# One core's decoder layer: negated rstd kept in the rstd's tile, first weights loaded ahead of x and the norm's scale, nine matmuls on zeros

## The chip, the cores and the metric

One core of a Trainium2 chip runs the whole layer. The metric is the time of one execution on the device in microseconds, of the slowest core, which here is the only one. Several executions are timed; one more is profiled, and all rows come from that one.

## The reference, cut to what matters

All tensors are float32; x is 512 x 2048.

```python
h = rms_norm(x, norm_gain)
q, k, v, g_attn, c_b, c_c, c_h, g_conv = split(h @ w_in)         # 2048 -> 6656
q, k = partial_rope(rms_norm(q, ...)), partial_rope(rms_norm(k, ...))
y_attn = sliding_window_attention(q, k, v, sinks) * silu(g_attn)  # 16 heads of 64, window 128
y_conv = c_b * short_conv(c_c * c_h, conv_w) * silu(g_conv)
x = x + concat(y_attn, y_conv) @ w_out                            # 2048 -> 2048
gate = sigmoid(rms_norm(x, ple_gate_norm_gain) @ w_ple_gate + b)  # 2048 -> 2048
x = x + gate * rms_norm(p @ w_ple_proj, ple_norm_gain)
```

## The kernel before

**Precision.** Every float32 operand is split into a high part, rounded to the matmul's own format, and the rest, the low part (`wh` and `wl` of weights, `hsh` and `hsl` of the normed x, `form` for both). One product is three matmuls: high by high, low by high, high by low.

**Stages.** The head (lines 262 to 283) loads x in 16 tiles of 128 x 512 and the weights of k and v in 16 pieces of 256 KB, scales each x tile by the norm's gain (`norm_g`, the norm's scale) and splits it, and gathers k and v in four banks of PSUM (L274: wh stationary, hsh or hsl moving). The rstd itself is only applied to the products. Then `gemm_tile` (L155 to L157) makes 24 tiles of the input projection, with weights from `wsp` stationary and hs from `hsp` moving; attention (L448, L449, transposes L481, values L495 and L496) and the embedding's projection (`e_block`, L555) run in between. From about 386 us on, seven groups of block products (L845, a scheme with seven products for a 2 x 2 block) make the rest of the input projection (groups 0 to 2), the output projection (3, 4) and the gate (5, 6). There `form`, 128 x 128 pieces of the activations, is stationary and `wh` or `wl`, 128 x 512, is moving. A step is one of the forms 1 to 7 for one of four chunks of the rows, 12 matmuls. In groups 0 to 2 the forms are pieces of hs: forms 1, 2, 4 and 7 lie in `hsp`, forms 5, 6 and 3 in `fx`, but forms 6 and 3 of chunk 3 lie in `rowp` (`h_slot("rows" if j > 5 else "fx")`, L1282).

**Order.** TensorE's instructions stand in the order of the code throughout. ScalarE's and VectorE's do so in the first six rounds of the head and again in the block products; between, a scheduler sets them. SyncE and GpSimd issue the loads and stores, each in one queue. In a round of the head ScalarE makes `hsh` (L133), casts `wh` (L117) and squares x; VectorE makes `hsl` (L134) and `wl` (L118). `fetch` (L97 to L107) issues the loads of x and weights.

**Memory.** A pool is a stretch of every partition; its place follows from the sizes of the pools ahead of it. `const`, `small`, `hsp`, `wsp`, `wraw` and what replaces them (`fx`, `tab`, `ap`, `cw`) are stacked from the left; `rowp`, `big`, and the block products' `spl`, `wx`, `wy`, `ws`, `io_p`, `quad` from the right end. `r_neg` (L301) is a tile of 32 floats in `const` of which four are used: the rstd of x times -1/8, which `x_squared` writes and GpSimd reads for the scale of q.

**Start.** TensorE begins with ten products of a tile of zeros by itself (L187, L188); each stands as two records in the trace.

Of the kernel before, what the change touches and what calls it, by code (L numbers as in the profile page):

```python
# [9 lines left out]
F32 = mybir.dt.float32  # L10
F32R = mybir.dt.float32r
AF = mybir.ActivationFunctionType
ALU = mybir.AluOpType

P = 128
# [3 lines left out]
NB = T // P  # L19
HD = 64  # L20
# [10 lines left out]
def f32(ap):  # L31
    return ap.bitcast(F32)
# [3 lines left out]
def hymba_layer(ctx: ExitStack, tc: tile.TileContext, io):  # L36
# [14 lines left out]
    nc = tc.nc  # L51
# [3 lines left out]
    const = ctx.enter_context(tc.tile_pool(name="const", bufs=1))  # L55
# [15 lines left out]
    def cload(name, shape):  # L71
        t = const.tile(shape, F32, name=name)
        nc.gpsimd.dma_start(t, io[name])
        return t
# [6 lines left out]
    jobs = [io["w_kv"][i] for i in range(8)]  # L81
# [5 lines left out]
    raws, splits = {}, {}  # L87
    RAW_AHEAD, SPLIT_AHEAD = 2, 3

    xt = []  # L90

    def load_x():
        xt.append(big.tile([P, T], F32, tag="big", name="x"))
        nc.sync.dma_start(xt[-1], io["x"][len(xt) - 1])

    def fetch(s):

        for j in range(min(s // 2 + RAW_AHEAD + 1, len(jobs))):
            if j not in raws:
                raws[j] = wraw.tile([P, 8, P], F32, name="raw")  # L100
                if j < 8:
                    for c in (slice(0, 4), slice(4, 8)):
                        load_x()
                        nc.sync.dma_start(raws[j][:, c], jobs[j][:, c])
                else:
                    nc.sync.dma_start(raws[j], jobs[j])

# [16 lines left out]
    def split_tile(src, scale=None, name="s", pool=None):  # L124

        pool, tag = (big, "big") if pool is None else (pool, "h")
        h = pool.tile([P, T], F32R, tag=tag, name=name + "h")
        l = pool.tile([P, T], F32R, tag=tag, name=name + "l")
        if scale is None:
            nc.scalar.copy(h, src)  # L130
            nc.vector.tensor_tensor(l, src, f32(h), op=ALU.subtract)
        else:
            nc.scalar.activation(h, src, AF.Copy, scale=scale)  # L133
            nc.vector.scalar_tensor_tensor(l, src, scale, f32(h), op0=ALU.mult, op1=ALU.subtract)  # L134
        return h, l
# [5 lines left out]
    def at(when, fn):  # L141
        later.append((when, len(later), fn))
# [41 lines left out]
    nc.vector.memset(zeros, 0.0)  # L184
    nc.scalar.activation(half_neg[:, 31:], zeros[:, :1], AF.Copy, bias=-0.5)
    warm_ps = ps_o.tile([P, P], F32, name="pso")
    for _ in range(10):  # L187
        nc.tensor.matmul(warm_ps, zeros, zeros, start=True, stop=True)  # L188

    ind = const.tile([P, 2 * P], F32R, name="ind")  # L190
    for c in range(2):
        nc.vector.tensor_copy(ind[:, c * P : (c + 1) * P], zeros)
    norm_g = const.tile([P, KT], F32, name="norm_gain")
    nc.sync.dma_start(norm_g, io["norm_gain"])
    ident = cload("ident", [P, P])
    gate_g = cload("ple_gate_norm_gain", [P, KT])
    qg, kg = cload("q_norm_gain", [P, 2]), cload("k_norm_gain", [P, 2])
# [4 lines left out]
    def half_sums(pm, hl, t, first, last):  # L202

        w = ind[:, P - 2 * t : 2 * P - 2 * t]
        nc.tensor.matmul(pm, w, hl[0], start=first, stop=False)
        nc.tensor.matmul(pm, w, hl[1], start=False, stop=last)

    def take_rows(pm, rows):
        sb = big.tile([rows, T], F32, tag="big", name="rowsum")
        nc.scalar.copy(sb, pm[:rows])  # L210
        return sb

    def to_tokens(sb):

        rows = sb.shape[0]
        pt = ps_m.tile([P, T], F32, name="psm")
        out = pt[:, : NB * rows].rearrange("p (b r) -> p b r", r=rows)
        for b in range(NB):
            nc.tensor.transpose(out[:, b, :], sb[:, b * P : (b + 1) * P], ident[:rows, :rows])
        return out  # L220

    def rstd(ms, n, out):

        nc.vector.tensor_scalar(ms, ms, 1.0 / n, EPS, op0=ALU.mult, op1=ALU.add)
        width = int(np.prod(ms.shape[1:]))
        e = half_neg[:, :width]
        if len(ms.shape) == 3:
            e = e.rearrange("p (a b) -> p a b", a=ms.shape[1])
        nc.gpsimd.tensor_tensor(out, ms, e, op=ALU.pow)

    tok = {}

    def token_rstd(name, sq, out, when):


        def sums():
            pm = ps_o.tile([P, T], F32, name="pso")
            half_sums(pm, hl, 0, True, True)
            tok["s"] = take_rows(pm, 2)

        def turn():
            ms = small.tile([P, NB], F32, name="ms")
            nc.vector.tensor_reduce(ms, to_tokens(tok["s"]), axis=mybir.AxisListType.X, op=ALU.add)
            r = tok[name] = const.tile([P, NB], F32, name="r_" + name)
            rstd(ms, D, r)
            tok["rb"] = big.tile([P, NB, P], F32, tag="big", name="rb")
            nc.vector.tensor_copy(tok["rb"], r.unsqueeze(2).broadcast_to([P, NB, P]))

        def rows():
            pb = ps_m.tile([P, T], F32, name="psm")  # L250
            for b in range(NB):
                nc.tensor.transpose(pb[:, b * P : (b + 1) * P], tok["rb"][:, b, :], ident)
            nc.scalar.copy(out, pb)

        hl = split_tile(sq)
        for stage, t in zip((sums, turn, rows), when):
            at(t, stage)
# [32 lines left out]

    def x_squared():
        nc.vector.tensor_tensor(rx2_tok, tok["x"], tok["x"], op=ALU.mult)
        nc.vector.tensor_scalar(r_neg, tok["x"], -(HD**-0.5), None, op0=ALU.mult)
        nc.vector.tensor_tensor(rx2, rx, rx, op=ALU.mult)

    c0 = clock[0]
    token_rstd("x", acc, rx, (c0 + 3, c0 + 5, c0 + 8))
    at(c0 + 9, x_squared)

    attn_dram = [dram.tile([2 * P, T], F32, name=f"a{j}") for j in range(NKV)]  # L300
    r_neg = const.tile([P, 32], F32, name="r_neg")[:, :NB]  # L301
    conv_dram, mix_dram = ([dram.tile([P, T], F32, name=f"{n}{i}") for i in range(8)] for n in ("c", "m"))

    with ExitStack() as att:
# [16 lines left out]
        def squares(ps):  # L321
            sq = big.tile([P, T], F32, tag="big", name="sqh")
            nc.scalar.activation(sq, ps, AF.Square)
            return sq

        def head_scale(rows, out, r, engine):

            shape = [P, NB, rows.shape[0]]
            ms = small.tile(shape, F32, name="msh")
            nc.vector.tensor_tensor(  # L330
                ms, to_tokens(rows), rx2_tok.unsqueeze(2).broadcast_to(shape), op=ALU.mult
            )
            rstd(ms, HD, ms)
            return lambda: engine.tensor_tensor(out, ms, r.unsqueeze(2).broadcast_to(shape), op=ALU.mult)

        def rotate(ps, g):
            t1 = big.tile([P, T], F32, tag="big", name="rot")
            sh = cw.tile([P, T], F32, tag="cw", name="shf", bufs=4)
            nc.vector.stream_shuffle(sh, ps, shuf)
            nc.vector.scalar_tensor_tensor(t1, ps, g[:, 0:1], cos, op0=ALU.mult, op1=ALU.mult)  # L340
            nc.vector.scalar_tensor_tensor(sh, sh, g[:, 1:2], sin, op0=ALU.mult, op1=ALU.mult)
            nc.vector.tensor_tensor(t1, t1, sh, op=ALU.add)
            return t1
# [68 lines left out]
        def q_tile(t):  # L412
            ps = product()
            sq = split_tile(squares(ps))

            def sum_q():
                if t % 4 == 0:
                    tok["q"] = ps_o.tile([P, T], F32, name="pso")
                half_sums(tok["q"], sq, t % 4, t % 4 == 0, t % 4 == 3)
                if t % 4 == 3:  # L420
                    tok["q"] = take_rows(tok["q"], 8)

            def scale_q():
                sl = nscale[:, :, 2 * t - 6 : 2 * t + 2]
                head_scale(tok["q"], sl, r_neg, nc.gpsimd)()

            at(clock[0] + 6, sum_q)
            if t % 4 == 3:
                at(clock[0] + (9 if t == 3 else 17), scale_q)
            qr = rotate(ps, qg)  # L430
            for hf in range(2):
                own, oth = slice(hf * HD, hf * HD + HD), slice((1 - hf) * HD, (1 - hf) * HD + HD)
                st = big.tile([P, T], F32R, tag="big", name="qst")
                nc.scalar.copy(st[own], qr[own])
                nc.vector.tensor_tensor(st[oth], qr[own], f32(st[own]), op=ALU.subtract)
                qst[2 * t + hf] = st
# [74 lines left out]
        def product():  # L511

            i = tile_at[0]
            tile_at[0] += 1
            ps = gemm_tile(hs, mid=(lambda: e_block(E_AT.index(i))) if i in E_AT else None)
            for fn in busy.pop(i, ()):
                fn()
            return ps
# [860 lines left out]
```

## Time and profile before

| what | value |
|---|---|
| median of 3 runs | 953.41 us (952.49 to 954.28) |
| the profiled execution, its own time | 952.76 us |
| its span, first to last instruction | 951.0 us |
| granted TensorE clock, mean | 0.999 |
| TensorE, matmuls | 943.8 us busy, 4294 records |
| VectorE | 711.2 us busy |
| ScalarE | 524.8 us busy |
| GpSimd | 151.2 us busy |
| memory read and written | 197 GB/s over the span |

A record of a matmul lasts from its start to its modelled end and overlaps the next one's, so the pace of a stream is read from the distance of starts: in the chain in order of time, each piece with its count runs to the start of the next.

### The profile page before, as it was taken

Reading aid. Unit: us, or ns where it says so; the run is one execution under the profiler, and the core shown is the slowest. Engines: PE = TensorE matmul, PEld = TensorE weight load, DVE = VectorE, ACT = ScalarE, POOL = GpSimd, SP = SyncE. Lnnn points to the kernel's source line nnn. Section 1 sums busy time; section 2 is a strip of 40 time slices with the busy share of each in tenths; the row PEclk is TensorE's granted clock in tenths of the full one; section 3 lists DMA queues with packets and bytes.
Section 4 is the critical chain, followed back from the end, with each engine's and each line's share of the span. In section 5 each row is a group of like instructions: output and inputs, shape, how many; then the busy total and the mean of one; then the engine's idle time right before and its main releaser. Section 6 shows DMA issues by size and latency. Waiting matters only on the chain.

```text
span 951.0 us, 12360 instructions
## 1 busy us (share of the span) xinstructions
PE 943.8 (99%) x4294; PEld 775.1 (82%) x4294; DVE 711.2 (75%) x1104; ACT 524.8 (55%) x891; POOL 151.2 (16%) x200
## 2 busy tenths in 40 slices
PE   9999999999999999999999999999999999999997
PEld 7888888888888888888888888888888888888886
DVE  6778867975766676667667768988858686997678
ACT  7546555665656665345344446555657566664453
POOL 2002142051212221000100110011020112002101
PEclk9999999999999999999999999999999999999999
DMA  9434455564555657765824887787996895579956
GB/s 318 143 103 155 144 192 199 175 187 101 150 160 147 195 154 257 267 222 195 225 74 159 277 203 223 239 236 177 272 313 171 224 294 129 133 234 303 223 136 210
DMA packets 68078, 188.22 MB, mean 198 GB/s; under 512 B 8144, under 2 KB 14592, under 8 KB 68016
## 3 DMA queue, kind: packets, MB, share of 16 engines
q1 hardware_dynamic: 46336, 128.48, 39.6%
q0 software_dynamic: 21680, 58.96, 27.1%
q8 instruction: 33, 0.54, 0.2%
q14 instruction: 29, 0.24, 0.1%
HBM read 158.05 MB, written 29.36 MB: 197 GB/s over the span
## 4 chain that ended last, share of the span: by engine, by line
PE 98%; DVE 0%; DMA 0%; ACT 0%; SPq 0%; issue 0%
PE psp L845 53%; PE psg L155 9%; PE psg L157 9%; PE psg L156 9%; PE pst L845 4%; PE pss L274 2%; PE pst L274 2%; PE pst L911 1%; PE pst L481 1%; PE pst L555 1%; PE pss L555 1%; PE pss L449 1%; PE pss L448 1%; PE pso L496 1%; PE pso L495 1%; DMA raw<-in_w_kv 0%
## 5 line engine op out<-in xcount | busy, mean ns | idle before, releaser
L845 PE MATMUL psp<-wh,form 128*128 128x512 f32 x1056 | 331.6, 395 | 0.0
L845 PEld LDWEIGHTS psp<-wh,form 128*128 128x128 f32 x1056 | 197.9, 188 | 45.4
L845 PE MATMUL psp<-wl,form 128*128 128x512 f32 x528 | 208.4, 395 | 0.0
L155 PE MATMUL psg<-hsh,wh 128*128 128x512 f32 x384 | 152.0, 396 | 0.0
L157 PE MATMUL psg<-hsh,wl 128*128 128x512 f32 x384 | 149.9, 390 | 0.0
L156 PE MATMUL psg<-hsl,wh 128*128 128x512 f32 x384 | 149.8, 390 | 0.0
L812 DVE TENSOR_TENSOR wl<-wy,wh 128x1024 fp32r<-128x1024 f32 x84 | 102.5, 1222 | 52.3 <-ACT wh L811 52.3
L811 ACT CAST wh<-wy 128x1024 fp32r<-128x1024 f32 x84 | 88.0, 1048 | 85.1 <-PE psp L845 62.9
L118 DVE TENSOR_TENSOR wl<-raw,wh 128x512 fp32r<-128x512 f32 x120 | 82.2, 687 | 49.5 <-ACT wh L117 31.1
L845 PEld LDWEIGHTS psp<-wl,form 128*128 128x128 f32 x528 | 99.4, 188 | 23.2
L117 ACT CAST wh<-raw 128x512 fp32r<-128x512 f32 x120 | 73.6, 617 | 68.6 <-PE psg L156 51.6
L812 DVE TENSOR_TENSOR wl<-wx,wh 128x1024 fp32r<-128x1024 f32 x56 | 68.4, 1223 | 35.9 <-ACT wh L811 35.8
L811 ACT CAST wh<-ws 128x1024 fp32r<-128x1024 f32 x56 | 58.8, 1051 | 62.9 <-PE psp L845 38.2
L811 ACT CAST wh<-wx 128x1024 fp32r<-128x1024 f32 x56 | 58.6, 1049 | 61.5 <-PE psp L845 52.7
L812 DVE TENSOR_TENSOR wl<-ws,wh 128x1024 fp32r<-128x1024 f32 x56 | 68.5, 1223 | 25.3 <-ACT wh L811 25.1
L157 PEld LDWEIGHTS psg<-hsh,wl 128*128 128x128 f32 x384 | 72.1, 188 | 15.4
L155 PEld LDWEIGHTS psg<-hsh,wh 128*128 128x128 f32 x384 | 72.2, 188 | 14.1
L156 PEld LDWEIGHTS psg<-hsl,wh 128*128 128x128 f32 x384 | 72.2, 188 | 13.9
L845 PE MATMUL psp<-wh,hsh 128*128 128x512 f32 x192 | 76.1, 396 | 0.0
L845 PE MATMUL psp<-wh,hsl 128*128 128x512 f32 x192 | 75.8, 395 | 0.0
L845 PE MATMUL psp<-wl,hsh 128*128 128x512 f32 x192 | 75.7, 394 | 0.0
L797 DVE TENSOR_TENSOR wy<-wy,ws 128x1024 f32<-128x1024 f32 x56 | 68.2, 1217 | 0.4 <-DMA ws<-in_w_ple_gate 0.4
(223 smaller groups left out, 1353.3 us busy)
## 6 DMA issues: line engine op xcount, KB each, us to landing
raw<-in_w_in SPq DMA_DIRECT2D x48, 512.0 KB, 3.5
ws<-in_w_mid SPq DMA_DIRECT2D x24, 512.0 KB, 4.0
h<-hf POOLq DMA_DIRECT2D x32, 256.0 KB, 4.4
wx<-in_w_mid SPq DMA_DIRECT2D x16, 512.0 KB, 4.2
wx<-in_w_out SPq DMA_DIRECT2D x16, 512.0 KB, 5.3
ws<-in_w_out SPq DMA_DIRECT2D x16, 512.0 KB, 5.4
ws<-in_w_ple_gate SPq DMA_DIRECT2D x16, 512.0 KB, 5.3
wy<-in_w_mid SPq DMA_DIRECT2D x12, 512.0 KB, 6.8
```

Source lines behind the costliest of these rows:

```text
L117: nc.scalar.copy(wh, raw)
L118: nc.vector.tensor_tensor(wl, raw, f32(wh), op=ALU.subtract)
L155: nc.tensor.matmul(ps, wh, ah, start=first, stop=False)
L156: nc.tensor.matmul(ps, wh, al, start=False, stop=False)
L157: nc.tensor.matmul(ps, wl, ah, start=False, stop=last)
L274: nc.tensor.matmul(kv_ps[t], w[:, t, :], a, start=k == 0 and i == 0, stop=k == KT - 1 and i == 2)
L448: nc.tensor.matmul(sc[:, r, lo:], q, khh[j][:, ks], start=True, stop=False)
L555: nc.tensor.matmul(banks[t], a, w, start=k == 0 and i == 0, stop=k == 1 and i == 2)
L797: tt(y, y, got[g, "s1" if f == 6 else "s0", c], op=ALU.add)
L811: nc.scalar.copy(wh, src)
L812: tt(wl, src, f32(wh), op=ALU.subtract)
L845: nc.tensor.matmul(ps[t], a, w[:, i], start=start and first and i == 0 and n == 0, stop=last and i == 1 and n == 2, skip_group_check=not s ...
```

## The change

Four edits. The negated and scaled rstd of x no longer has a tile of its own; it is the second half of the rstd's tile, which takes 32 bytes instead of 16 in a slot of 32. In each round of the head the weights' load is issued ahead of x's. The norm's scale is loaded by the same queue after the first x tile instead of ahead of everything. There are nine matmuls on zeros instead of ten.

```diff
@@ fetch
                     for c in (slice(0, 4), slice(4, 8)):
+                        nc.sync.dma_start(raws[j][:, c], jobs[j][:, c])
                         load_x()
-                        nc.sync.dma_start(raws[j][:, c], jobs[j][:, c])
+                        if len(xt) == 1:
+                            nc.sync.dma_start(norm_g, io["norm_gain"])
@@ hymba_layer
-    for _ in range(10):
+    for _ in range(9):
         nc.tensor.matmul(warm_ps, zeros, zeros, start=True, stop=True)
...
     norm_g = const.tile([P, KT], F32, name="norm_gain")
-    nc.sync.dma_start(norm_g, io["norm_gain"])
@@ token_rstd, turn
-            r = tok[name] = const.tile([P, NB], F32, name="r_" + name)
+            both = const.tile([P, 2 * NB], F32, name="r_" + name)
+            r = tok[name] = both[:, :NB]
+            tok[name, -1] = both[:, NB:]
@@ x_squared
-        nc.vector.tensor_scalar(r_neg, tok["x"], -(HD**-0.5), None, op0=ALU.mult)
+        nc.vector.tensor_scalar(tok["x", -1], tok["x"], -(HD**-0.5), None, op0=ALU.mult)
@@ hymba_layer
-    r_neg = const.tile([P, 32], F32, name="r_neg")[:, :NB]
@@ scale_q
-                head_scale(tok["q"], sl, r_neg, nc.gpsimd)()
+                head_scale(tok["q"], sl, tok["x", -1], nc.gpsimd)()
```

Where the built programs put the tiles, in bytes from the start of a partition, and what is left when the address is divided by 256:

| pool | tiles of a matmul | first before | mod 256 | first after | mod 256 |
|---|---|---|---|---|---|
| `const` | `ident` | 17760 | 96 | 17760 | 96 |
| `hsp` (left) | hsh, hsl, form | 20320 | 96 | 20192 | 224 |
| `wsp` (left) | wh, wl of the head, `gemm_tile`, `e_block` | 85856 | 96 | 85728 | 224 |
| `fx` (left) | form | 85856 | 96 | 85728 | 224 |
| `tab` (left) | vv | 119648 | 96 | 119520 | 224 |
| `ap` (left) | prob, pth_a, ptl_a | 128096 | 96 | 127968 | 224 |
| `big` (right) | ptsh, ptsl, qst and others | 157664 | 224 | 157664 | 224 |
| `spl` (right) | wh, wl of the block products | 163808 | 224 | 163808 | 224 |
| `quad` (right) | z, x2 | 126944 | 224 | 126944 | 224 |
| `rowp` (right) | form of chunk 3 | 221152 | 224 | 221152 | 224 |

The tiles of these pools, `const` apart, are whole multiples of 256 bytes long, and a matmul takes them whole or in pieces of 512 or 2048 bytes, so the remainder holds for each of its operands. Apart from the head the five engines' instructions keep their order.

SyncE, the start of the program; `raw` is a piece of the weights, `x` a tile of x. Before:

```order
L194 DMA norm_gain<-in_norm_gain 128x16
L94 DMA x<-in_x 128x512
L104 DMA raw<-in_w_kv 128x512
L94 DMA x<-in_x 128x512
L104 DMA raw<-in_w_kv 128x512
```

and now:

```order
L103 DMA raw<-in_w_kv 128x512
L94 DMA x<-in_x 128x512
L106 DMA norm_gain<-in_norm_gain 128x16
L103 DMA raw<-in_w_kv 128x512
L94 DMA x<-in_x 128x512
```

The scale has moved from the first place to the third, and in each pair the weights stand first.

ScalarE, the first two rounds of the head; DMAHW0, 1, 2 and so on are the semaphores of SyncE's loads in the order in which they are issued. Before:

```order
L133 ACTIVATE hsh<-x,norm_gain 128x512 [waits DMAHW1_49,DMAHW0_49]
L117 CAST wh<-raw 128x512 [waits DMAHW2_49]
L278 ACTIVATE acc_x<-x 128x512
L133 ACTIVATE hsh<-x,norm_gain 128x512 [waits DMAHW3_49]
L117 CAST wh<-raw 128x512 [waits DMAHW4_49]
```

and now:

```order
L135 ACTIVATE hsh<-x,norm_gain 128x512 [waits DMAHW2_49,DMAHW1_49]
L119 CAST wh<-raw 128x512 [waits DMAHW0_49]
L281 ACTIVATE acc_x<-x 128x512
L135 ACTIVATE hsh<-x,norm_gain 128x512 [waits DMAHW4_49]
L119 CAST wh<-raw 128x512 [waits DMAHW3_49]
```

Nothing has moved on ScalarE; the first instruction waits for the second and third load instead of the first and second.

## Rows read from the trace of the kernel before

**Rows 1.** Page, parts 1 and 2: TensorE's busy time; its granted clock in slices.

```profile
PE 943.8 (99%) x4294; PEld 775.1 (82%) x4294; DVE 711.2 (75%) x1104; ACT 524.8 (55%) x891; POOL 151.2 (16%) x200
PEclk9999999999999999999999999999999999999999
```

**Rows 2.** Chain that ended last, by line: share of the span.

```profile
by line: PE psp L845 52.8%; PE psg L155 9.3%; PE psg L157 9.2%; PE psg L156 9.2%; PE pst L845 4.4%; PE pss L274 2.4%; PE pst L274 2.3%; PE pst L911 1.5%; PE pst L481 1.3%; PE pst L555 1.2%; PE pss L555 1.2%; PE pss L449 0.8%; PE pss L448 0.
```

**Rows 3.** Groups by line: tiles, shapes, count | busy us, mean ns | idle.

```profile
L845 PE MATMUL psp<-wh,form 128*128 128x512 f32 x1056 | 331.6, 395 | 0.0
L845 PE MATMUL psp<-wl,form 128*128 128x512 f32 x528 | 208.4, 395 | 0.0
L845 PE MATMUL psp<-wh,hsh 128*128 128x512 f32 x192 | 76.1, 396 | 0.0
L845 PE MATMUL pst<-wh,form 128*128 128x512 f32 x128 | 40.2, 395 | 0.0
L481 PE MATMUL pst<-ident,prob 128*128 128x128 f32 x112 | 15.0, 273 | 0.0
L911 PE MATMUL pst<-ident,z 128*128 128x128 f32 x64 | 8.3, 272 | 0.0
```

**Rows 4.** Chain in order of time around the quick stretches: start us, us, what.

```profile
423.58 5.72 PE psp L845 x25
...
497.75 5.58 PE psp L845 x24
503.33 5.69 PE psp L845 x25
508.80 5.81 PE psp L845 x25
```

**Rows 5.** Chain in order of time, other lines.

```profile
20.43 0.45 PE pss L274 x2
...
116.49 2.80 PE pss L555 x12
...
226.37 0.23 PE pso L495
...
227.05 0.23 PE pso L496
```

**Rows 6.** Timeline of the start: start us, us, engine, line, operation [idle before <-releaser].

```profile
0.73 0.39 SPq L194 DMA_DIRECT2D norm_gain<-in_norm_gain  x1
...
1.09 4.63 PE L188 MATMUL pso<-zeros 128*128 128x128 f32 x20 [1.09 <-DVE zeros L184]
...
1.17 0.42 SPq L94 DMA_DIRECT2D x<-in_x  x1
...
1.64 0.42 SPq L104 DMA_DIRECT2D raw<-in_w_kv  x1
...
4.07 0.72 ACT L133 ACTIVATE hsh<-x,norm_gain 128x512 fp32r<-128x512 f32 x1 [1.54 <-DMA x<-in_x]
...
5.52 0.62 ACT L117 CAST wh<-raw 128x512 fp32r<-128x512 f32 x1 [0.73 <-DMA raw<-in_w_kv]
...
6.19 1.08 PE L274 MATMUL pss<-hsh,wh 128*128 128x512 f32 x2 [0.47 <-ACT wh L117]
...
7.11 0.63 PE L274 MATMUL pst<-hsh,wh 128*128 128x512 f32 x2
```

**Rows 7.** DMA issues in two short windows: tiles, queue, count, KB, us to landing.

```profile
x<-in_x SPq DMA_DIRECT2D x1, 256.0 KB, 2.8
...
raw<-in_w_kv SPq DMA_DIRECT2D x1, 256.0 KB, 3.9
```

**Rows 8.** Timeline near 643; windows: us, busy of PE, PEld, DVE, ACT, POOL.

```profile
642.67 0.41 DVE L577 TENSOR_TENSOR form<-raw,form 128x256 fp32r<-128x256 f32 x1
...
643.23 0.64 PE L845 MATMUL psp<-wh,form 128*128 128x512 f32 x2
...
800.00:850.00 50.00, 50.00 (x217) 40.53 (x216) 46.15 (x60) 31.12 (x40) 4.92 (x5) 1.00 0.51 151
```

## The prediction

> **What bounds the kernel now.** I read the busy rows of the page first. TensorE is busy for 943.8 of the 951.0 us of the span [rows 1]. So an edit pays only if it changes TensorE's own pace, its first real matmul or the tail; a shorter wait on another engine is worth nothing.
>
> The chain by line says where the pace is to be looked for [rows 2]: `psp L845`, the block products of the second half, holds 52.8% of the span, 502 us. The groups of that line count 1056 + 528 + three times 192 = 2160 matmuls into `psp` (and 128 + 64 into `pst`), all 128 x 512 [rows 3]. 502.1 / 2160 = 232.5 ns from one start to the next. (The mean of 395 ns in those rows is the length of one record, which overlaps the next; it isn't the pace.)
>
> Then the chain in order of time, in short windows. In the middle of L845, 25 matmuls from 503.33 take 5.69 us, 227.6 ns each. The 24 just before them take 5.58 us (232.5 each) and the 25 just after 5.81 (232.4). There are three such quick stretches; the one at 583 has the same 5.69 for 25, the one at 423.58 has 5.72 (228.8 each) [rows 4]. Line, shapes and neighbours in time are alike. What differs is where the stationary operand lies: these are steps 6 and 3 of chunk 3 in groups 0 to 2, whose `form` tiles are in `rowp` and not in `hsp` or `fx`. By the table of addresses in the section on the change, `rowp` and the moving tile in `spl` both start 224 bytes past a multiple of 256, `hsp` and `fx` 96 past one.
>
> The other combinations are there too [rows 5]. Both operands at 96: L274 does two matmuls in 0.45 us, and L495 and L496 (`ap` moving, `vv` or `wsp` as the next stationary) take 0.23 each. Moving at 96, stationary at 224: L555 needs 2.80 us for 12, 233 ns. So 96 with 96 is quick, 224 with 224 quick, 224 with 96 slow, 96 with 224 slow. My reading: while a matmul streams its moving operand, the next one's stationary operand is loaded, and a pair whose addresses differ by 128 modulo 256 costs 4 to 6 ns more.
>
> **The change part by part.**
> *128 bytes.* `r_neg` took 128 bytes in `const`, and every pool that is allocated from the left stands behind it. Without it they all drop by 128; the pools on the right stay. Left tiles go from 96 to 224: left with left stays equal, right with right stays equal, left with right becomes equal. In L845 the 2160 + 192 = 2352 matmuls less three stretches of 24 leave 2280 that change from slow to quick. The slow pace without those 72: (502.1 - 72 x 0.228) / 2088 = 232.6 ns. The quick pace in the same line is (5.69 + 5.69 + 5.72) / 75 = 228.0. 2280 x 4.6 ns = 10.5 us. L555 (96 matmuls) gains 96 x 4.6 ns = 0.4 us. The transposes of L481, against `ident`, which stays put, become unequal. I cost that at nothing: 1.3% of the span for 112 of them is 0.11 us each, and 1.5% for the 128 of L911, unequal already, is 0.11 too [rows 2, 3]; at most it would be 112 x 4.6 ns = 0.5. **Gain 10.9 us.** Ends: with the slowest of the quick stretches, 228.8, it is 2280 x 3.8 ns = 8.7; with the pace of L274, about 227, it is 2280 x 5.6 + 0.5 = 13.3. I take the middle, because it comes from the same line.
>
> The Trainium skill says otherwise. "TensorE: Matmul & The Clock Gate", section "Step-by-step: what each phase is for", gives TensorE two independent read ports: "Loading the next tile's weights doesn't steal SBUF read bandwidth from the running matmul." By that no address could matter and this part would be worth 0 in place of 10.9; the two paces inside one line [rows 4] speak against it.
>
> *Start.* Before, SyncE issues the norm's scale at 0.73, x at 1.17, the first weights at 1.64; ScalarE makes `hsh` at 4.07, waits 0.73 for the weights, casts `wh` at 5.52, and TensorE starts at 6.19 [rows 6]. From their issues x took 2.8 us to land and the weights 3.9 [rows 7], so they were there at about 4.0 and 5.5. Now the weights go first, x second, the scale third; but ScalarE's order is unchanged, `hsh` ahead of `wh`. So `hsh` waits for the scale, which is behind both big loads, and `wh`, though its weights are there, is queued behind `hsh`; VectorE's `hsl` and `wl` and all of TensorE wait for that. Weights: 0.73 + 2.8 = 3.5. x as second load of 256 KB: as the second landed before, 5.5, less the 0.45 by which the loads start sooner, so about 5.0; the ends are 4.2 (half of that distance behind the weights) and 5.5 (nothing sooner). The scale, 8 KB behind it, lands 0 to 0.2 later. `hsh` starts at 4.2 to 5.7, I take 5.1, and TensorE 0.72 + 0.62 + 0.05 later: 6.5 (5.6 to 7.1). That is 0.3 later (-0.6 to +0.9). The first two matmuls are slow before (0.92 us to the third's start at 7.11, against 0.45 for a pair later); if that slowness ends at the same moment, a later start loses only half, so **+0.2 us**.
>
> *Nine matmuls on zeros.* One less is 2 of 20 records, 4.63 / 20 x 2 = 0.46 us [rows 6]; they end near 5.3 instead of 5.7. They stand beside the wait for the loads, so this takes nothing off the path. With the start above, TensorE's pause ahead of L274 grows from 0.47 to about 1.2 us. The granted clock stands at full (2.4 GHz) in all slices [rows 1]; only the slow first matmuls hint at the lower level (1.2 GHz) before, and a longer pause might hold that longer (rival C).
>
> *The rest.* `x_squared` writes the same four columns into another tile, GpSimd reads them there: nothing. SyncE's later loads swap within pairs: nothing, since the second `wh` is needed only 12 matmuls (2.7 us) after the first.
>
> *Who is late next.* A stream 2% quicker meets VectorE. The tightest spot: `form` L577 is made from 642.67 to 643.08, and TensorE goes on at 643.23 with it, 0.15 us to spare [rows 8]. VectorE's work just ahead of that is let go by TensorE's transposes some 7 us earlier, so TensorE gains 7 x 2% = 0.14 on it: no stall, barely. VectorE is fullest from 800 to 850, 46.15 of 50 us [rows 8]; the loss there is between 0 (if TensorE's buffers let go each run) and 50 x 2% = 1.0. I take **+0.3**, since 3.85 us of idle time are left.
>
> **Sum.** 952.76 - 10.9 + 0.2 + 0.3 = 942.4 for the profiled execution. That execution is 0.65 below the median of the runs, 953.41; for a median the same change gives **943.0 us**.
>
> **The rivals.**
> *A, some of it is given back.* VectorE becomes the bound in the full stretches, 570 to 650 and 800 to 900: TensorE gains 180 x 2% = 3.6 us there; if it loses all of that again, 946.6. Against: TensorE shows no such wait now, and VectorE still has idle time in its fullest 50 us.
>
> *B, the address isn't the cause.* In all rows the quick pairs also lie on one side of the memory and the slow ones on opposite sides. If the side decides, the 128 bytes do nothing and only the start is left: 953.41 + 0.2 = 953.6. For it: no pair of opposite sides with equal addresses exists in this trace. Against: `ap` lies past the middle of the partition, its partners `vv` and `wsp` before it, and L495 and L496 are quick; a dividing line would have to lie in the 13 KB between `ap` and `big`. By the Trainium skill's sentence on the two read ports, quoted above, the time would be the one of this rival too.
>
> *C, slower.* Place: the first two instructions of the head on ScalarE. `hsh` waits for the scale until 5.7, TensorE starts 0.9 later than now, and the longer pause keeps it at the slow pace for as long again as from the first zeros to 7.11, 6 us at half pace: +3.0. It decides only if the gain from the addresses is under about 2 us, so it needs B as well: 953.41 + 0.9 + 3.0 = 957.3. Without B it only moves my forecast to some 946.5.
>
> **How the numbers follow.** Forecast 0.78, A 0.06, B 0.12, C 0.04. Low end: the gain of 13.3 with nothing given back and the start 0.5 better, 939.6. High end: the gain of 8.7 with the start 0.9 and VectorE 1.0 worse is 946.6; a bit more, to 947.5, takes in A and the long pause. From 939.5 to 947.5 it leaves out B, C and a little of the forecast, 2 in 10. A measurement here can tell about 0.2%, 1.9 us, from no change: forecast and A are faster, 0.84; B is the same, 0.12; C slower, 0.04.
>
> **What would show it.** Right: `psp L845` falls from 502 us to about 492, 25 matmuls take 5.7 us everywhere in that line, L555 12 in 2.73, while L274 and L495 stay. TensorE's idle time stays where it is. The start: `hsh` near 5.1, let go by the scale's load, `wh` right behind it, TensorE near 6.5, zeros until 5.3. Wrong: L845 still at 232 ns (B); waits of TensorE for `wl` or `form` between 570 and 900 (A); pairs of L274 at 0.9 us until 10 us or later (C).

## The result and the profile after

The changed kernel takes 942.46 us in the median of four runs (942.31 to 944.45); the kernel before, on the same chip, 952.95 (952.39 to 954.28). The ratio is 0.9893, 95% interval 0.9875 to 0.991. The forecast was 943.0, in a range of 939.5 to 947.5. The profiled execution took 942.31, 10.45 less than that of before. All lines have moved by two or three numbers: L845 is L847 now, L555 L557, L274 L277, L495 and L496 are L497 and L498, L811 is L813.

The page of the kernel after, its lines that answer to [rows 1] and [rows 3]:

```profile
PE 930.5 (99%) x4292; PEld 772.7 (82%) x4292; DVE 710.3 (76%) x1104; ACT 525.8 (56%) x891; POOL 151.1 (16%) x200
...
PEclk9999999999999999999999999999999999999999
...
L847 PE MATMUL psp<-wh,form 128*128 128x512 f32 x1056 | 326.6, 390 | 0.9 <-DVE form L579 0.9
...
L847 PE MATMUL psp<-wl,form 128*128 128x512 f32 x528 | 205.6, 389 | 0.5 <-DVE wl L814 0.5
```

TensorE has 13.3 us less work at the same share of the span, and the mean record of L847 is 5 ns shorter. The idle column was 0.0 in these two rows before [rows 3] and is 1.4 us now.

The chain that ended last, in order of time (start us, us, what; the five longest pieces):

```profile
384.85 84.34 PE psp L847 x372
473.69 73.46 PE psp L847 x324
551.63 54.42 PE psp L847 x240
638.66 67.39 PE psp L847 x296
789.34 51.71 PE psp L847 x228
```

All give 226.7 to 227.7 ns for one matmul. The first piece contains the stretch of [rows 4] at 423, and it is one piece: the quick stretches no longer stand out, because everything is as quick. The other lines of [rows 5], the chain in short windows:

```profile
20.28 0.45 PE pss L277 x2
...
116.87 2.77 PE pss L557 x12
...
226.38 0.23 PE pso L497
226.61 0.23 PE pso L498
```

L557 went from 2.80 to 2.77 us for this dozen, and over all its pairs, by the distances between starts in the trace, from 232.6 to 227.2 ns a matmul. L277 and L497/L498, equal before and after, have not moved.

The start, from the timeline of the kernel after (start us, us, engine, line, operation [idle before <-releaser]), as in [rows 6]:

```profile
0.73 0.39 SPq L103 DMA_DIRECT2D raw<-in_w_kv  x1
...
1.09 4.21 PE L190 MATMUL pso<-zeros 128*128 128x128 f32 x18 [1.09 <-DVE zeros L186]
...
1.65 0.42 SPq L106 DMA_DIRECT2D norm_gain<-in_norm_gain  x1
...
5.60 0.72 ACT L135 ACTIVATE hsh<-x,norm_gain 128x512 fp32r<-128x512 f32 x1 [3.07 <-DMA norm_gain<-in_norm_gain]
...
6.23 0.60 ACT L119 CAST wh<-raw 128x512 fp32r<-128x512 f32 x1
...
6.88 0.74 PE L277 MATMUL pss<-hsh,wh 128*128 128x512 f32 x2 [1.59 <-ACT wh L119]
```

`hsh` is let go by the norm's scale, 1.53 us later than before, `wh` follows with no wait of its own, and TensorE starts 0.69 later. In the second round `hsh` waits for its x, which now stands behind the weights in the queue. Before:

```profile
7.23 0.72 ACT L133 ACTIVATE hsh<-x,norm_gain 128x512 fp32r<-128x512 f32 x1 [0.56 <-DMA x<-in_x]
```

and after:

```profile
8.68 0.72 ACT L135 ACTIVATE hsh<-x,norm_gain 128x512 fp32r<-128x512 f32 x1 [1.32 <-DMA x<-in_x]
```

TensorE's 13th matmul of the head then starts 0.42 us behind the 12th instead of 0.23.

**Where the 10.45 us came from.** The distances from one TensorE start to the next, summed by line: L847 with its waits left out 12.7 us less, L557 0.53, the transposes L483 0.13 less. Against that, the 49th matmul of the head starts 0.75 later (18.31 instead of 17.55), two waits in L847 take 2.03, and the tail behind the last matmul 0.23 more. 13.4 - 3.0 = 10.4.

The two waits, which no row of before has. TensorE at 638, then ScalarE ahead of that:

```profile
637.36 0.39 PE L847 MATMUL psp<-wh,form 128*128 128x512 f32 x1
638.66 0.50 PE L847 MATMUL psp<-wh,form 128*128 128x512 f32 x1 [0.91 <-DVE form L579]
...
629.35 1.05 ACT L813 CAST wh<-wy 128x1024 fp32r<-128x1024 f32 x1 [3.09 <-DMA wy<-in_w_out]
```

Before, ScalarE waited for the same block as well, but for less long, and TensorE did not stop:

```profile
633.62 1.05 ACT L811 CAST wh<-wy 128x1024 fp32r<-128x1024 f32 x1 [2.22 <-DMA wy<-in_w_out]
```

The second wait, at 873, in the chain in order of time of the kernel after:

```profile
866.94 5.54 DMA wy<-in_w_ple_gate
...
872.56 1.06 ACT wh L813
...
873.64 1.24 DVE wl L814
...
874.92 5.30 PE psp L847 x22
```

TensorE stands behind VectorE (`form`, `wl`), but VectorE was itself waiting for ScalarE's cast, and that for a block of weights into which GpSimd's queue adds a second block by DMA. The releaser named last is VectorE; the late one is the transfer.

### The profile page after: what moved, and what is told of

Read it like the earlier page. It is cut to its first block, busy times and chain, and to the rows that moved or that the text cites. A ratio compares the mean times of both kernels' runs of the same rounds, so it can differ in the third digit from the quotient of the medians.

```text
span 940.5 us, 12355 instructions
## 1 busy us (share of the span) xinstructions
PE 930.5 (99%) x4292; PEld 772.7 (82%) x4292; DVE 710.3 (76%) x1104; ACT 525.8 (56%) x891; POOL 151.1 (16%) x200
## 2 busy tenths in 40 slices
DMA packets 68078, 188.22 MB, mean 200 GB/s; under 512 B 8144, under 2 KB 14592, under 8 KB 68016
## 4 chain that ended last, share of the span: by engine, by line
PE 91%; DMA 4%; DVE 3%; issue 1%; ACT 1%; SPq 0%; DVEq 0%; ACTq 0%; POOLq 0%
PE psp L847 47%; PE psg L157 9%; PE psg L159 9%; PE psg L158 9%; PE pss L277 2%; DMA wy<-in_w_ple_gate 2%; PE pst L277 2%; PE pst L847 2%; PE pst L483 1%; PE pst L913 1%; PE pss L557 1%; PE pst L557 1%; DMA wy<-in_w_out 1%; DVE wl L814 1%; DVE z L1156 1%
## 5 line engine op out<-in xcount | busy, mean ns | idle before, releaser
L847 PE MATMUL psp<-wh,form 128*128 128x512 f32 x1056 | 326.6, 390 | 0.9 <-DVE form L579 0.9
L847 PEld LDWEIGHTS psp<-wh,form 128*128 128x128 f32 x1056 | 197.3, 188 | 41.9 <-DVE form L579 1.3
L847 PE MATMUL psp<-wl,form 128*128 128x512 f32 x528 | 205.6, 389 | 0.5 <-DVE wl L814 0.5
L813 ACT CAST wh<-wy 128x1024 fp32r<-128x1024 f32 x84 | 88.3, 1052 | 82.4 <-PE psp L847 58.8
L847 PEld LDWEIGHTS psp<-wl,form 128*128 128x128 f32 x528 | 99.1, 188 | 21.6 <-DVE wl L814 1.0
L813 ACT CAST wh<-ws 128x1024 fp32r<-128x1024 f32 x56 | 59.1, 1055 | 58.4 <-PE psp L847 35.5
L813 ACT CAST wh<-wx 128x1024 fp32r<-128x1024 f32 x56 | 58.9, 1053 | 57.2 <-PE psp L847 49.1
L847 PE MATMUL psp<-wh,hsh 128*128 128x512 f32 x192 | 75.0, 391 | 0.0
L847 PE MATMUL psp<-wl,hsh 128*128 128x512 f32 x192 | 74.7, 389 | 0.0
L847 PE MATMUL psp<-wh,hsl 128*128 128x512 f32 x192 | 74.7, 389 | 0.0
```

Of the source, the lines that this page charges most:

```text
L813: nc.scalar.copy(wh, src)
L847: nc.tensor.matmul(ps[t], a, w[:, i], start=start and first and i == 0 and n == 0, stop=last and i == 1 and n == 2, skip_group_check=not s ...
```

## The experiments

All runs stand beside runs of the kernel before on the same chip (952.82, 952.68, 952.31 and 952.86 us in the four groups). The trace's line numbers differ by one or two between the kernels; L845, L846 and L847 are the same matmul.

### The pools alone, the start alone

The first is the kernel before with the negated rstd in the rstd's tile and nothing else; the second the kernel before with nothing else but

```diff
-                        load_x()
                         nc.sync.dma_start(raws[j][:, c], jobs[j][:, c])
+                        load_x()
+                        if len(xt) == 1:
+                            nc.sync.dma_start(norm_g, io["norm_gain"])
...
-    for _ in range(10):
+    for _ in range(9):
```

> The kernel before with the negated rstd in the rstd's tile alone: left pools 128 bytes lower, start as before. Address theory (a pair whose addresses differ by 128 modulo 256 is slow): the block products at 226.8 ns a matmul as in the changed kernel, 941.7 us, that is the changed kernel's 942.46 less the 0.75 by which its 49th matmul of the head starts later than before (18.305 against 17.552). If the pace came from the new start instead: block products at 232.5, 952.9.

> The kernel before with the new order of loads and nine matmuls on zeros alone, pools where they were. Address theory: block products stay at 232.5 ns, first real matmul near 6.9, 49th near 18.3, 953.7 us (before 952.95 + 0.75). If the new start were a gain: under 952.9.

Pools alone: 940.59 us (938.94 to 943.47), ratio 0.9874 (0.9856 to 0.9893), L845 at 226.8 ns over all its pairs. Start alone: 953.44 (952.27 to 955.75), ratio 1.0007 (0.9999 to 1.0016), L845 at 232.3. The chain in one window of L845, first the pools alone, then the start alone:

```profile
514.83 15.19 PE psp L846 x67
```

```profile
514.94 15.10 PE psp L846 x65
```

The whole gain comes from the pools; the new start is worth nothing or a small loss. The two taken apart also show how much a start scatters: with the same code `hsh` began at 4.65 in the second run and at 5.60 in the kernel after, in both let go by the scale.

### The pools 128 bytes higher

```diff
-    r_neg = const.tile([P, 32], F32, name="r_neg")[:, :NB]
+    r_neg = const.tile([P, 64], F32, name="r_neg")[:, :NB]
```

> The kernel before with r_neg of 64 floats in place of 32, so that the left pools lie 128 bytes higher, and nothing else. Address theory: left with right is equal modulo 256 again, block products at 226.8 ns, 941.7 us. Rivals: what counts is that the pools lie lower, or on which side of the memory a tile lies: 232.5 ns, 952.9 us or more.

940.87 us (940.49 to 941.33), ratio 0.9874 (0.9861 to 0.9888), 226.8 ns over all pairs. The same window:

```profile
514.81 15.41 PE psp L845 x68
```

Moving up by 128 does what moving down does. A place that is lower, or memory that was freed, is not the cause.

### The right side moved instead

The mirror image: 128 bytes are left free at the right end, so `spl`, `rowp` and `big` move and the left pools stay at 96.

```diff
+    ctx.enter_context(tc.tile_pool(name="gap", bufs=1, side="right")).tile([P, 32], F32, name="gap")
     rowp = ctx.enter_context(tc.tile_pool(name="rowp", bufs=4, side="right", reuse_waits="tile"))
```

> The kernel before with 128 bytes left free at the outer end of the right side, so that the right pools (the moving operands' spl, rowp, big) move by 128 bytes and the left pools stay at 96 modulo 256: the distance is 0 with the left pools where they were. Theory, the distance modulo 256 sets the pace: 226.8 ns at L845, about 941. Rival, the left pools' own place (96 modulo 256) is the slow one: 232.5 ns, about 953.

941.37 us in one run. The chain in a window of L845 without quick stretches, first the kernel before:

```profile
514.84 15.33 PE psp L845 x66
```

and this kernel:

```profile
514.94 15.19 PE psp L846 x67
```

232.3 ns against 226.7. The left operands stand where they stood, so it isn't their place that is slow; the right ones stood at 224 in the pools alone, which was quick, so it isn't theirs either; and the two operands still lie on opposite sides. It is their distance. Rival B is out.

### 32, 64 and 96 bytes instead of 128

The edit is the one above with 24, 16 and 8 floats for `r_neg`. The left pools then lie at 64, 32 and 0 modulo 256, and the moving operand of L845 starts 160, 192 and 224 bytes past the stationary one modulo 256 (128 in the kernel before, 0 after). In L555, where the sides are swapped, it starts 96, 64 and 32 past it.

> The kernel before with its tile r_neg 24 floats wide instead of 32: the pools of the left side lie 32 bytes lower (weights' stage wsp at 64 modulo 256, the other side's at 224), so the stationary and the moving operands of the 128x512 matmuls start 160 (or 96) bytes apart modulo 256, against 128 before and 0 after. Theory 1, only a distance of 128 modulo 256 costs: pace of line L845 226.8 ns, time about 941. Theory 2, every distance other than 0 costs the same: 232.5 ns, about 953. Theory 3, the cost falls as the distance leaves 128 (from 232.5 at 128 to 226.8 at 0, in a straight line): about 231 ns, 950. The rival that it is the lower place as such, and not the distance, would give 232.5 here too, since 32 bytes lower changes the place least.

> The kernel before with r_neg 16 floats wide: the left pools lie 64 bytes lower (at 32 modulo 256), a distance of 192 (or 64). Theory 1 (128 alone costs): 226.8 ns at L845, about 941. Theory 2 (every distance but 0 costs): 232.5 ns, about 953. Theory 3 (straight line): 229.7 ns, about 947.

> The kernel before with r_neg 8 floats wide: the left pools lie 96 bytes lower (at 0 modulo 256), a distance of 224 (or 32). Theory 1 (128 alone costs): 226.8 ns, about 941. Theory 2 (every distance but 0): 232.5 ns, about 953. Theory 3 (straight line): 228.2 ns, about 944. The three runs with 32, 64 and 96 bytes and the two at 0 and 128 that are there give the curve; line L555, where both kinds of operands change sides, is a second reading of it.

One run each: 956.43, 953.41 and 954.11 us. The same window of the chain, for 32 bytes:

```profile
514.78 15.23 PE psp L845 x65
```

for 64:

```profile
514.97 15.17 PE psp L845 x65
```

for 96:

```profile
514.98 15.17 PE psp L845 x65
```

That is 234.3, 233.4 and 233.4 ns. Over all pairs of the program, from the starts in the trace (ns, mean from one start to the next; the pools in brackets are the moving and the next stationary operand's):

| distance mod 256 | L845 (`spl`, `hsp`) | distance mod 256 | L555 (`wsp`, `big`) |
|---|---|---|---|
| 0 | 226.8 | 0 | 227.2 |
| 224 | 233.3 | 32 | 233.2 |
| 192 | 233.2 | 64 | 229.2 |
| 160 | 234.1 | 96 | 233.4 |
| 128 | 232.6 | 128 | 232.6 |

The theory that only 128 costs falls, and so does the straight line. Of the distances tried, all multiples of 32, only equal remainders are quick; each of the others costs about the same, 128 the least in L845. One value stays by itself, the 229.2 at 64 in L555, from 91 pairs. That the modulus is 256 and not 512 follows from the pools alone and the pools higher: their left sides are 256 bytes apart, and both are quick. That the next matmul's stationary operand counts, and not the running one's, can be read from before: in each of the three quick stretches the last matmul, whose own operand is in `rowp` and the next one's in `hsp`, took 232 or 233 ns.

### Fewer transfers

The kernel after, with the sums of two groups of weights made by VectorE instead of by the adding DMAs, twelve transfers of a 128 x 1024 block less (the expectation counts sixteen; the page has 181.92 MB moved instead of 188.22):

```diff
-    T1_BY_DMA, T3_BY_DMA = range(1, NG), (2, 3, 4)
+    T1_BY_DMA, T3_BY_DMA = range(1, NG - 1), (2, 4)
```

> The changed kernel with the sums of the last group (y + x for form 5) and the differences of group 3 (form 7) made on VectorE, as group 0 makes them, in place of transfers that add in memory: 8 transfers of 512 KB less for the last group and its first block (4 accumulating ones), 8 for group 3, 4 more VectorE instructions of 1.22 us in each. Theory that late transfers caused the two new pauses of TensorE at 637.4 (1.07 us) and 873 to 874 (0.96 us): both gone, 940.4 us. Rival, VectorE's own work caused them: the pause at 637 stays, and the one at 874 grows, 942.5 or more.

941.71 us (940.5 to 942.05), ratio 0.9879 (0.9864 to 0.9894). Both waits are gone: at 638 TensorE runs through,

```profile
637.78 0.62 PE L847 MATMUL psp<-wh,form 128*128 128x512 f32 x2
638.24 0.40 PE L847 MATMUL psp<-wl,form 128*128 128x512 f32 x1
638.48 0.62 PE L847 MATMUL psp<-wh,form 128*128 128x512 f32 x2
...
628.46 1.05 ACT L813 CAST wh<-wy 128x1024 fp32r<-128x1024 f32 x1 [2.29 <-DMA wy<-in_w_out]
```

and from the 49th matmul to the last it takes 913.6 us, 2.3 less than the kernel after, with more work on VectorE. So it isn't the load on VectorE that makes TensorE wait; that the transfers do is borne out by a table in the part on why the prediction was right. The profiled execution is only 0.36 below that of the kernel after (941.95): its 49th matmul came 0.45 later, and from the last matmul to the end it took 7.81 us instead of 6.29 (more on that with the last run). The timeline of its head:

```profile
5.86 1.22 PE L277 MATMUL pss<-hsh,wh 128*128 128x512 f32 x2 [0.56 <-ACT wh L119]
6.88 1.05 PE L277 MATMUL pst<-hsh,wh 128*128 128x512 f32 x2
7.73 1.05 PE L277 MATMUL pss<-hsl,wh 128*128 128x512 f32 x2
8.59 1.05 PE L277 MATMUL pst<-hsl,wh 128*128 128x512 f32 x2
9.44 0.82 PE L277 MATMUL pss<-hsh,wl 128*128 128x512 f32 x2
10.10 0.63 PE L277 MATMUL pst<-hsh,wl 128*128 128x512 f32 x2
10.56 0.62 PE L277 MATMUL pss<-hsh,wh 128*128 128x512 f32 x2
```

Until 9.86, pairs start 0.85 us apart, 427 ns a matmul, and then 0.46. That is the slow pace of rival C, though TensorE started 1.0 us earlier than in the kernel after and had stood idle for 0.56 us instead of 1.59. The run with the right side moved had the same until 10.7, with the old start and its ten matmuls on zeros. So it comes with either start. It is the lower clock: in the trace's record of the granted clock the stretch at the full level begins at 9.86 us here and at 10.69 there, where the slow pace ends. Over all fourteen profiled executions it begins between 4.27 and 10.69, in the kernel before at 6.98, inside its slow first two matmuls, and in the kernel after at 6.03, while TensorE stood idle between the zeros and the head.

### The norm's scale on ScalarE's queue

The kernel after with another start: the scale goes first on a queue of its own, x and then the weights on SyncE's.

```diff
+    norm_g = const.tile([P, KT], F32, name="norm_gain")
+    nc.scalar.dma_start(norm_g, io["norm_gain"])
...
-    for _ in range(9):
+    for _ in range(8):
```

> The kernel after with another start: the norm's scale is loaded first on ScalarE's own queue, x and then the first weights on SyncE's, in the written order, and eight matmuls on zeros instead of nine. If the start's price is the late landing of the scale behind raw and x (5.51 us in the kernel after, hsh at 5.60, TensorE at 6.88): x lands at about 3.5, raw at about 4.4, TensorE begins at about 5.1 and the 49th matmul of the head at about 16.9 (18.31 after, 17.55 before), a time 1.4 us below the kernel after, about 941.1; with the same pause of 2 us at 638 and 873. The rival: the scale's landing isn't the bound, hsh then waits for x and ScalarE, TensorE begins at 5.6 or later and the time stays within 0.5 us of 942.4. Against both: the earlier end of the zeros leaves TensorE at half the granted clock for its first matmuls (427 ns each instead of 227), which takes back about 1.5 us.

940.88 us (939.56 to 941.8), ratio 0.9874 (0.9858 to 0.9891). Timeline of ScalarE and TensorE:

```profile
3.76 0.72 ACT L133 ACTIVATE hsh<-x,norm_gain 128x512 fp32r<-128x512 f32 x1 [0.80 <-DMA norm_gain<-in_norm_gain]
4.39 0.60 ACT L117 CAST wh<-raw 128x512 fp32r<-128x512 f32 x1
...
5.04 1.22 PE L276 MATMUL pss<-hsh,wh 128*128 128x512 f32 x2 [0.17 <-ACT wh L117]
6.06 1.04 PE L276 MATMUL pst<-hsh,wh 128*128 128x512 f32 x2
6.92 0.65 PE L276 MATMUL pss<-hsl,wh 128*128 128x512 f32 x2
```

`hsh` 1.84 us sooner than in the kernel after, TensorE at 5.04 (5.1 expected), the 49th matmul at 16.94 (16.9 expected), and 1.6 us off the time. The first four matmuls pay with the slow pace. In the three profiled kernels with this start TensorE begins the head at 4.93 to 5.09, in the eleven others at 5.65 to 6.88. Whether the scale's queue or x's first place does it was not tested apart. And by the medians it only brings back the old start: 940.88 against 940.59 for the pools alone. Two waits of 1.0 us together are left at 871.

### The versions put together

Two kernels: this start with fewer transfers, and the pools alone (old start) with fewer transfers. (The expectation words the second edit badly: what it moves is the sums of weights, from DMA to VectorE.)

> The start of the run with the scale on ScalarE's queue (TensorE at 5.05 us, the 49th matmul of the head at 16.94) together with the two half-products' terms taken from TensorE's side instead of by DMA (the run with fewer transfers, whose pauses at 638 and 873 us were gone: 913.6 us from the 49th matmul to the last, against 915.9 in the kernel after). If both are independent: last matmul at 16.94 + 913.6 = 930.5, a time of about 939.2, 3.2 below the kernel after and 1.7 below the run with the start alone. If the late transfers are merely put off, the pauses return at another place and the time stays at 940.9.

> The pools alone (start of the kernel before, ten matmuls on zeros) with fewer transfers. If the changed start is worth nothing or a small loss: the 49th matmul at 17.1 to 17.5, the last at about 931, a time of about 939.6; the kernel after with fewer transfers gave 941.7, so a difference of some 2 us would be the price of the new start when the clock stays low in it. If the start of the kernel before keeps TensorE's first four or nine matmuls at the lower clock too, 941 to 942.

939.88 us (939.13 to 941.56), ratio 0.9864 (0.9845 to 0.9883), and 940.05 (939.68 to 941.85), ratio 0.9866 (0.985 to 0.9882). Neither has a wait in L845. The first has TensorE at 5.09 and takes 914.0 us from the 49th matmul to the last, as expected; the second was profiled in its slowest run, with TensorE idle for 1.64 us in the second round of the head, until the weights were there. In the first, two delays of 0.1 us at 636 are left. In both, the end came 1.1 to 1.2 us later behind the last matmul than in the kernel after, so some of what the waits had cost went there. GpSimd's last drain, an instruction at the end of the program, lasts 7.9 and 7.8 us in them instead of 3.6.

### The sums of the last group alone

The start with the scale on ScalarE's queue, and of the two sums only the last group's on VectorE:

```diff
-    T1_BY_DMA, T3_BY_DMA = range(1, NG), (2, 3, 4)
+    T1_BY_DMA, T3_BY_DMA = range(1, NG - 1), (2, 3, 4)
```

> The start with the scale on ScalarE's queue, and VectorE in place of the adding DMAs for the sums of the last group alone (the two edits together also took group 3's). In the three runs with both edits the program's end came 7.4 to 7.8 us after TensorE's last matmul, against 6.3 in the others at the quick pace: GpSimd's last drain took 7.8 us in place of 3.6 to 3.9. If group 3's edit is what makes that drain long: drain near 3.8, end 6.3 us after the last matmul, the wait at 871 gone, a time of about 939.0 to 939.9. If the last group's edit is: drain near 7.8, end 7.4 behind the last matmul, about 940.9.

939.06 us (938.64 to 941.23), ratio 0.9862 (0.9846 to 0.9879). No wait is left in L846, at 638 neither, and the long end is still there: drain 7.95 us, 7.57 us from the last matmul to the end. The drain ends at 936.76, behind SyncE's at 935.43, which is the later one in the kernel after (939.70 against 937.71). So the last group's edit is what lengthens the end, by 1.3 us; how the drain comes to last longer where GpSimd issues fewer adding DMAs was not found. This is the quickest of all kernels run. All its four runs lie below the fastest of the kernel after, 942.31, but the intervals of the two ratios overlap.

All profiled executions side by side, from the starts in the trace: the first matmul of the head, its 49th, the waits in L845 (delays under 0.114 us left out), and from the start of the last matmul to the end, all in us.

| kernel | start | first | 49th | waits | end |
|---|---|---|---|---|---|
| before | old | 6.19 | 17.55 | 0 | 6.06 |
| 32, 64, 96 bytes | old | 6.65, 5.90, 6.35 | 17.67, 16.91, 17.41 | 0, 0, 0 | 6.07, 6.06, 6.04 |
| start alone | new | 5.93 | 17.51 | 0.26 | 6.04 |
| after | new | 6.88 | 18.31 | 2.03 | 6.29 |
| pools alone | old | 6.05 | 17.07 | 1.04 | 6.28 |
| pools higher | old | 5.65 | 17.04 | 1.38 | 6.28 |
| right side moved | old | 6.23 | 19.31 | 0 | 6.29 |
| scale on ScalarE's queue | third | 5.05 | 16.94 | 1.02 | 6.29 |
| fewer transfers | new | 5.86 | 18.75 | 0 | 7.81 |
| both | third | 5.09 | 16.48 | 0 | 7.47 |
| pools, fewer transfers | old | 6.04 | 19.03 | 0 | 7.38 |
| last group's sums | third | 4.93 | 16.23 | 0 | 7.57 |

## Why the prediction was right, and where its steps were not

**The pace: right cause, too small a term, too narrow a rule.** The gain was put at 10.9 us and came out at 13.2 (12.7 in L847, 0.5 in L557), at the upper end of 13.3. The step that failed is the quick pace of 228.0 ns. It was read from the 25-matmul pieces of [rows 4], whose edges hold matmuls between `rowp` and `hsp` or `fx`; by the starts in the trace of before, those with `rowp` as their own and the next operand ran at 227.5, since a stretch needs up to eight matmuls of 224 to 236 ns to settle; the 15 that stand last among them ran at 226.7 in each of the three. That is the pace after the change. The pairs of L274, 226.7 as well, were the better measure, and stood as the other end. The rule "differ by 128 modulo 256" fitted all rows of before, which held only the distances 0 and 128. The runs with 32, 64 and 96 bytes show that any unequal remainder costs 6 to 7 ns in L845.

**Rival B** fell with the kernel after, and with the right side moved: opposite sides, equal remainders, quick. The Trainium skill's sentence in "TensorE: Matmul & The Clock Gate", section "Step-by-step: what each phase is for", that loading the next weights doesn't take read bandwidth from the running matmul, would leave the addresses without effect. Here they have an effect: 232.6 against 226.8 ns for the same instructions. The measurement decides; what in the memory collides was not measured.

**The start.** The order of events was right (`hsh` let go by the scale, `wh` right behind, zeros until 5.3), the size half right. `hsh` was put at 5.1 and TensorE at 6.5; the three profiled executions with this start had 5.60, 4.65 and 4.58, and 6.88, 5.93 and 5.86. In the kernel after, the 49th matmul was 0.75 us late, against +0.2 forecast. The first came 0.69 later; the first round then ran 0.31 quicker, since the two slow matmuls were gone; the second lost 0.37, because its x landed later. That last loss is a term that the prediction had put at nothing ("SyncE's later loads swap within pairs"); with the start alone TensorE began that round 0.42 us late as well. By the medians of runs the new start costs 0.6 (alone), 1.9 (after against pools alone) and 1.7 us (with fewer transfers). Each of these carries an uncertainty of one to two microseconds, but all three have the same sign, and the run with the scale on its own queue takes as much back. In the profiled executions TensorE begins at 6.23 on average with the new start and at 6.13 with the old, and reaches the 49th at 18.19 against 17.75. So the term is a loss, probably of more than 0.2 us; its size is not settled.

**Nine matmuls on zeros:** 4.21 us for 18 records, off the path, as forecast. **L481:** unequal now, and 97.8 instead of 98.9 ns; nothing, as forecast.

**Who is late next** was the step with the wrong owner. VectorE was put at +0.3 us, with `form` at 643 as the tightest place. TensorE did stop at that `form` (638.66 after), but for a transfer. In the four full-transfer kernels at the quick pace other than the one with the right side moved, the waits are 1.0 to 2.0 us; at the slow pace 0 to 0.26; with fewer transfers 0, in four kernels. They follow how late the transfer is. For the block of the second wait (873 in the kernel after), in the ten executions that bring it by adding DMAs:

| ScalarE's wait for the block, us | kernels | TensorE's wait, us |
|---|---|---|
| 1.77 | before | 0 |
| 2.21 to 2.55 | 96, 64, 32 bytes; pools alone (2.38) | 0 |
| 2.65 | right side moved | 0 |
| 3.06 | start alone | 0.26 |
| 3.60 | after | 0.96 |
| 3.77 | scale on ScalarE's queue | 1.02 |
| 4.13 | pools higher | 1.38 |

At 638 TensorE stops in the two executions in which ScalarE had waited for 3.09 (after) and 3.73 us (pools alone), and hardly or not in the others, with 2.91 or less. Read as a cost of this change, that is 2.0 in the profiled execution, and about 1 in the others. The likely reason for the later landing is that the same bytes have to land in a stretch that is 2% shorter; it is not shown. From 610 to 630 the share of the DMA engines is 0.99 instead of 0.89 (277 GB/s instead of 239), though the two windows don't hold quite the same work, since the kernel after is 5.7 us further on. Why the blocks came early enough at 638 with the right side moved, at a share of 1.01, and with the last group's edit alone, which leaves the transfers of group 3 as they were, stays open; with one profiled execution each it may be chance. So that it was the edit which took the wait at 638 away isn't shown.

The errors cancelled: 2.3 us more gain from the pace, 0.6 and 1.7 us more loss at the start and behind transfers. The cause of the gain was right; that the forecast met the result to half a microsecond was luck.

**Rival C's mechanism** exists, the slow pace until 10 us, but it was seen with either start and not behind the longest pause (1.59 us in the kernel after, with no slow matmul behind it), and it costs 1.2 to 1.8 us at the 49th matmul (18.75 and 19.31 against 17.55), not the 3.0 that was put down.

## What to carry to other kernels

Where a stream of matmuls loads a new stationary operand for each of them, look at the start addresses of both operands modulo 256 in the built program: a tile of a few bytes in an early pool decides it for all that lie behind, and padding to equal remainders cost nothing and gave 2.5% of the stream's time here. Read the quick pace from matmuls whose neighbours are all quick. Leave out the first ones behind each change of neighbours as well. And when the bound engine gets faster, look at what lands just in time for it, and follow the chain one step further back than the engine that the wait names.

## What the runs showed of the hardware

- A 128 x 512 matmul with a new stationary operand took 226.7 ns from start to start where moving and stationary operands start at equal remainders modulo 256, and 232.6 to 234.1 in L845 where they don't. Equal remainders aren't all of it: in the kernel after, the 16 matmuls of L847 that stand ahead of the 128 x 128 transposes of L913, whose stationary operand is a tile of `quad` at an equal remainder, took 232.4. Why was not tried.
- An 8 KB load landed 1.6 or 1.7 us after its issue as the first load of SyncE's queue (eight executions), 2.8, 2.9 and 3.9 us as the third, behind two of 256 KB, and 2.9 to 3.0 us as the only one on ScalarE's queue, as the rows of the DMA issues have it. So its place in the queue isn't all that counts. In the kernel after, first in the start and then, for comparison, of the kernel with the scale on ScalarE's queue:

```profile
norm_gain<-in_norm_gain SPq DMA_DIRECT2D x1, 8.0 KB, 3.9
```

```profile
norm_gain<-in_norm_gain ACTq DMA_DIRECT2D x1, 8.0 KB, 3.0
```

- TensorE's first matmuls of the head ran at 427 ns until 9.86 and 10.7 us in two executions; in the others the slow pace ended before the head or within its first few matmuls, with eight to ten products of zeros ahead in all of them. The ratio to the quick pace is nearly that of its two levels, 1.2 and 2.4 GHz, and the slow pace ends where the trace's record of the granted clock has the full level begin. The windows of the profile print a granted clock of 1.00 in those stretches all the same, so there the pace tells more than that column.
